# Splitting the head weights of the next phases ahead of time, and keeping the parts in DRAM

## The chip, the cores and the metric

The kernel runs on one core of one Trainium2 chip, in one launch. The metric is the device time of an execution, in microseconds (us). Beside the time there is one profiled execution, whose span is read through its page and its trace. The engines are PE (TensorE), DVE (VectorE), ACT (ScalarE), POOL (GpSimd) and SP (SyncE, which issues the transfers here).

## What is computed

Two layers of a decoder trunk, each made of feed-forward, mixer, feed-forward: six sub-layers on 512 tokens of 1024 features, all in float32. Each has the same frame, and the modulation (shift, scale, gate) comes from a product of a conditioning vector with `ada_w`:

```python
def _sublayer(x, fn, pre_g, post_g, shift, scale, gate, res_w):
    h = _rmsnorm(x, pre_g) * (1.0 + scale[:, None, :]) + shift[:, None, :]
    y = _rmsnorm(fn(h), post_g)
    return x + res_w * (1.0 + gate[:, None, :]) * y
```

`fn` is `(silu(h @ w1) * (h @ w3)) @ w2` with 2816 hidden features in the feed-forwards, a recurrence beside a convolution in the first layer's mixer (AB), and spatial gating in the second's (C). So two norms stand between any two sub-layers: one of the output, one of the sum that it is added to.

## The kernel before

**Phases.** The six sub-layers are phases 0 to 5: FFN, mixer AB, FFN, FFN, mixer C, FFN. Features lie on the partitions in eight tiles of 128 (`KT`), the 512 tokens on the free axis. PE multiplies in a 32-bit form of fewer mantissa bits, so each float32 product is made of three (`mm3`, L252 to L256): high part of the weight by high part of the value, low by high, high by low.

**Weights.** Each weight tile is loaded whole by SP's queue into one of four `raw` buffers (`fetch_w`, L228 to L231), and split on the chip into a high part (`wh`, ACT, L236) and a low part (`wl`, usually DVE, L237). There are eight buffers of each part. SP's queue works in the order in which the transfers were written.

**A feed-forward.** 22 pairs of hidden tiles in three chunks of 7, 7 and 8 (`CHUNKS`); after each chunk the products with w2 (`down`). A pair ends with its evacuation (L453 to L455, then the split at L246 and L247). Beside the products, *background jobs* run: one of the list `bg` in each *slot* (`run_bg`, called after a weight tile of a pair and after each w2 tile), and what is left at the end of the phase's body at once. Before, they are all blocks of the modulation: a load of 128x1024 of `ada_w` into a `raw` buffer and a DVE product with sum (`ada_block`, L136 to L138). There are 56 in phase 0, 24 in phase 2, 48 in phase 3.

**A change of phase.** The last seven output tiles of a phase are made in two halves of 256 tokens (`tail`), so that the norms of the first half run beside the products of the second. The norms are a chain (`chain`, L340 on): sums of squares (squares on ACT, L319; additions on GpSimd, L323, the last ones on DVE, L321), a product that gives the statistic (L287), the inverse root on DVE (L264 to L277, eight small operations), a product that spreads it over the partitions (L297), the scaled output (L354) added to x (L361), and then the same again for the next norm, up to h in two parts (L332 to L334). PE's own order is fixed, so that at each of these products it waits if DVE is late. Then the *head* of the next phase: its first three pairs of products (in C all of its first product), contraction tile by tile, on each half. The head's eight weight tiles (128x768, in C 128x1024) are fetched and split at the change itself, each as soon as PE releases buffers of the tail. The low parts of tiles 0 and 4 to 7 (`HP`) are split by GpSimd; those of 1 to 3 by DVE as "fills" at three places of the chain (`FILL`): behind the first spread, between the last two late additions, behind the second statistic.

Of the kernel before, what the change touches and what calls it, by code (L numbers as in the profile page):

```python
# [33 lines left out]
# AB: how long its steps wait, in microseconds of products; the output gates come after these square roots  # L34
# [4 lines left out]
# between phases: contraction tiles of the next weights split on GpSimd, splits that fill the gaps of the  # L39
# norms' chain (DVE, GpSimd), lag of the low parts, additions of squares that DVE takes, waits  # L40
HP = (0, 4, 5, 6, 7)
FILL, FILLG = (1, 1, 1, 0), (1, 2)
# [3 lines left out]
# start: products that warm the array, where c is spread, contraction tiles taken part by part  # L46
# [23 lines left out]
def trunk_kernel(ctx: ExitStack, tc: tile.TileContext, a: dict, out: bass.AP):  # L70
# [5 lines left out]
    ps = ctx.enter_context(tc.tile_pool(name="ps", bufs=1, space=bass.MemoryType.PSUM))  # L76

# [93 lines left out]
    def run_bg(n=1):  # L171
        for _ in range(n):
            if bg:
                if fence[0] is None:
                    bg.pop(0)()
                else:
                    with tc.issue_after(fence[0]):
                        bg.pop(0)()

# [1 line left out]
    class Flow:  # L181
        def __init__(self):
            self.t, self.gens, self.fills, self.pool, self.busy = 0.0, [], [], [], False
# [32 lines left out]
        def fill(self, n=1, m=0):  # L216
            for q, c in ((self.fills, n), (self.pool, m)):
                for _ in range(c):
                    if q:
                        q.pop(0)[1]()  # L220
# [11 lines left out]

    def split_w(raw, cols, eng):
        wh = sb.tile([P, 1024], F32R, tag="wh", bufs=8, name=nm("wh"))
        wl = sb.tile([P, 1024], F32R, tag="wl", bufs=8, name=nm("wl"))
        S.activation(wh[:, :cols], raw[:, :cols], AF.Copy)  # L236
        low = lambda e: e.tensor_tensor(wl[:, :cols], raw[:, :cols], wh[:, :cols].bitcast(F32), op=SUB)  # L237
        if eng in (1, 2):
            (flow.fills if eng == 1 else flow.pool).append((wh, lambda: low(V if eng == 1 else G)))
        else:  # L240
            low(eng)
        return wh, wl
# [17 lines left out]
    def rsqrt(src, scale):  # L260
        # first guess from the exponent bits, then a quartic in its residue
# [18 lines left out]
    # per token 1 / sqrt(mean over features + eps), on every partition  # L280
# [23 lines left out]
    class SumSq:  # L304
        # sums of squares over the feature tiles; the last ones wait for finish()
# [954 lines left out]
```

## Time and profile before

| | |
|---|---|
| three runs | 1930.12, 1931.41 (median), 1934.15 us |
| the profiled execution, its span | 1934.6 us |
| instructions | 24434 |
| DMA, mean over the span | 129 GB/s |
| read from HBM, written | 245.59 MB, 2.10 MB |

The profiled execution gives its span, and this lies 3.2 us above the median of the runs. A row of a profile names the line, the engine, the operation, and the output and inputs by their names in the program; "mm<-hid,wh" is a product into the PSUM tile `mm`. In brackets stands the time for which the engine was idle before the row, and what ended that. PE's rows overlap, so that their distance, and not their length, is the time that each takes. "PEclk" is the share of PE's full clock that was granted.

### The profile page before, as it was taken

How to read it: one execution, taken by the hardware profiler on the slowest of the kernel's cores; microseconds unless marked ns; L12 is line 12 of the kernel's file. 1: busy time of each engine (PE TensorE's matmuls, PEld its weight loads, DVE VectorE, ACT ScalarE, POOL GpSimd, SP SyncE). 2: the span in 40 equal slices, each digit the busy share in tenths (PEclk: the TensorE clock that was granted, in tenths of full speed). 3: DMA queues.
4: the chain of work that ended last, by engine and by line, in shares of the span. 5: the costliest groups of instructions: out<-in, count | busy, mean ns of one | idle time of the engine just before them, and what ended most of it. 6: DMA issues, size and time to landing. Idle time of an engine off the chain costs nothing.

```text
span 1934.6 us, 24434 instructions
## 1 busy us (share of the span) xinstructions
PE 1856.5 (96%) x9534; PEld 1567.5 (81%) x9534; DVE 1144.1 (59%) x1951; ACT 659.4 (34%) x1008; POOL 239.3 (12%) x200
## 2 busy tenths in 40 slices
PE   8999999988889999999989999999899999999997
PEld 5788888987568978888889788888878898888887
DVE  7985664687975775433367755553786483243334
ACT  3332222346755332222233322222334452222221
POOL 3200000237504000000040000000400410000002
PEclk8999999999889999999999999999999999999998
DMA  8486663421122286233222865643214132323311
GB/s 310 155 286 196 195 200 117 139 84 65 33 96 89 77 275 201 84 106 98 82 63 83 283 209 174 203 156 99 77 55 131 51 109 93 104 83 108 98 44 44
DMA packets 73125, 249.28 MB, mean 129 GB/s; under 512 B 8113, under 2 KB 10289, under 8 KB 73010
## 3 DMA queue, kind: packets, MB, share of 16 engines
q1 hardware_dynamic: 73010, 247.72, 39.3%
q8 instruction: 75, 1.23, 0.3%
q14 instruction: 40, 0.33, 0.1%
HBM read 245.59 MB, written 2.10 MB: 128 GB/s over the span
## 4 chain that ended last, share of the span: by engine, by line
PE 77%; DVE 13%; DMA 4%; ACT 3%; issue 2%; POOL 1%; SPq 0%; DVEq 0%; ACTq 0%; POOLq 0%
PE mm L256 24%; PE mm L254 24%; PE mm L255 24%; DMA raw<-in_w_dram 1%; DMA raw<-in_w13r_dram 1%; DVE wl L237 1%; DVE acc L321 1%; DVE ad L138 1%; DVE hl L334 1%; ACT wh L236 1%; PE st L297 1%; POOL hid L651 1%; POOL acc L323 1%; DVE mm L663 1%; DVE y L354 1%
## 5 line engine op out<-in xcount | busy, mean ns | idle before, releaser
L254 PE MATMUL mm<-hh,wh 128*128 128x512 f32 (+1 forms) x1734 | 644.2, 372 | 4.8 <-ACT hh L333 4.8
L256 PE MATMUL mm<-hl,wh 128*128 128x512 f32 (+1 forms) x1734 | 639.6, 369 | 0.6
L255 PE MATMUL mm<-hh,wl 128*128 128x512 f32 (+1 forms) x1734 | 637.8, 368 | 0.0
L236 ACT ACTIVATE wh<-raw 128x1024 fp32r<-128x1024 f32 (+2 forms) x310 | 313.8, 1012 | 512.0 <-PE mm L256 273.1
L254 PE MATMUL mm<-hid,wh 128*128 128x256 f32 (+1 forms) x1164 | 390.6, 336 | 5.2 <-ACT hid L246 3.3
L255 PE MATMUL mm<-hid,wl 128*128 128x256 f32 (+1 forms) x1164 | 387.9, 333 | 0.0
L256 PE MATMUL mm<-hid,wh 128*128 128x256 f32 (+1 forms) x1164 | 386.8, 332 | 0.2 <-DVE hid L247 0.2
L237 DVE TENSOR_TENSOR wl<-raw,wh 128x1024 fp32r<-128x1024 f32 (+2 forms) x277 | 327.5, 1183 | 99.7 <-ACT wh L236 98.3
L254 PEld LDWEIGHTS mm<-hh,wh 128*128 128x128 f32 x1734 | 327.5, 189 | 64.1 <-ACT hh L333 6.0
L255 PEld LDWEIGHTS mm<-hh,wl 128*128 128x128 f32 x1734 | 326.7, 188 | 60.1 <-issue 2.1
L256 PEld LDWEIGHTS mm<-hl,wh 128*128 128x128 f32 x1734 | 327.0, 189 | 58.7 <-DVE hl L334 1.9
L254 PEld LDWEIGHTS mm<-hid,wh 128*128 128x128 f32 x1164 | 223.6, 192 | 29.1 <-ACT hid L246 4.3
L256 PEld LDWEIGHTS mm<-hid,wh 128*128 128x128 f32 x1164 | 223.4, 192 | 23.4 <-DVE hid L247 1.2
L255 PEld LDWEIGHTS mm<-hid,wl 128*128 128x128 f32 x1164 | 223.8, 192 | 21.3
L138 DVE SCALAR_TENSOR_TENSOR raw<-raw,cb 128x1024 f32<-128x1024 f32 x128 | 156.1, 1223 | 139.1 <-DMA raw<-in_ada_w_dram 138.9
L237 POOL TENSOR_TENSOR wl<-raw,wh 128x768 fp32r<-128x768 f32 (+1 forms) x33 | 76.7, 2325 | 1091.4 <-ACT wh L236 794.7
L323 POOL TENSOR_TENSOR acc<-acc,tmph 128x256 f32<-128x256 f32 x112 | 90.4, 812 | 529.0 <-ACT tmph L319 521.8
L454 DVE SCALAR_TENSOR_TENSOR tmp<-tmp,mm 128x512 f32<-128x512 f32 x78 | 53.5, 686 | 147.3 <-ACT tmp L453 147.2
L455 DVE SCALAR_TENSOR_TENSOR tmp<-tmp,mm 128x512 f32<-128x512 f32 x78 | 53.5, 686 | 131.7 <-PE mm L256 131.4
L453 ACT ACTIVATE tmp<-mm 128x512 f32<-128x512 f32 x78 | 46.5, 596 | 243.1 <-PE mm L256 243.1
L482 DVE TENSOR_TENSOR y<-y,mm 128x256 f32<-128x256 f32 (+1 forms) x92 | 48.0, 522 | 123.5 <-PE mm L256 123.4
L651 POOL TENSOR_TENSOR hid<-hid,cp 128x507 f32<-128x507 f32 (+10 forms) x44 | 67.2, 1529 | 58.8 <-ACT cp L650 56.2
(204 smaller groups left out, 1317.0 us busy)
## 6 DMA issues: line engine op xcount, KB each, us to landing
raw<-in_w13r_dram SPq DMA_DIRECT2D x150, 512.0 KB, 3.8
raw<-in_ada_w_dram SPq DMA_DIRECT2D x128, 512.0 KB, 4.2
raw<-in_w_dram SPq DMA_DIRECT2D x64, 448.0 KB, 3.9
raw<-in_w_dram SPq DMA_DIRECT2D x32, 512.0 KB, 3.5
raw<-in_w13h_dram SPq DMA_DIRECT2D x24, 384.0 KB, 3.0
ad<-in_ada_w_dram SPq DMA_DIRECT2D x16, 512.0 KB, 7.2
raw<-in_ab_r_dram SPq DMA_DIRECT2D x10, 512.0 KB, 3.5
raw<-in_w13h_dram SPq DMA_DIRECT2D x8, 512.0 KB, 6.9
```

What stands on the lines that cost most here:

```text
L138: V.scalar_tensor_tensor(w, w, 0.5, cb, op0=MUL, op1=MUL, accum_out=modc[:, i : i + 1])
L236: S.activation(wh[:, :cols], raw[:, :cols], AF.Copy)
L237: low = lambda e: e.tensor_tensor(wl[:, :cols], raw[:, :cols], wh[:, :cols].bitcast(F32), op=SUB)
L254: PE.matmul(o, lhsT=wh, rhs=hi, start=start, stop=False, skip_group_check=shared)
L255: PE.matmul(o, lhsT=wl, rhs=hi, start=False, stop=False, skip_group_check=shared)
L256: PE.matmul(o, lhsT=wh, rhs=lo, start=False, stop=stop, skip_group_check=shared)
L323: G.tensor_tensor(self.acc, self.acc, t, op=ADD)
L453: S.activation(t, g, AF.Tanh, scale=0.5)
L454: V.scalar_tensor_tensor(t, t, 1.0, g, op0=ADD, op1=MUL)
L455: V.scalar_tensor_tensor(t, t, 0.5, u, op0=MUL, op1=MUL)
L482: V.tensor_tensor(self.ys[f][:, lo:hi], self.ys[f][:, lo:hi], o, op=ADD)
L651: G.tensor_tensor(ap[:, s:], ap[:, s:], q[:, s:], op=ADD)
```

## The change

A class `Ready` gives each head two steps. `prepare` returns eight background jobs; each loads a weight tile of the head, splits it (ACT and DVE, as for any weight) and stores both parts into tiles in DRAM. `bring(k)` loads the two parts of tile k from there into `wh` and `wl` buffers. Phase 0 prepares the heads of 1 and 2, phase 2 that of 3, phase 3 those of 4 and 5 (`KEEP`). At a change no weight is split: the fills, the list `HP`, and GpSimd's part are gone. The head of phase 0 is still split at the start, on GpSimd.

The jobs of a phase are merged evenly (`merge`), and spread evenly over its slots (`set_slots`), so that some slots take two. Some blocks of the modulation move to other phases (`MODS`): phase 0 has 48 blocks and 16 prepared tiles over 46 slots, phase 2 has 32 and 8 over 48, phase 3 has 40 and 16 over 48, phase 5 has 8 blocks. The rest of the diff takes comments away. Its core:

```diff
+MODS = {0: ((1, (1, 0, 2)), (2, (1, 0))), 2: ((2, (2,)), (3, (1, 0, 2))), 3: ((4, (1, 0, 2)), (5, (1, 0))), 5: ((5, (2,)),)}
+KEEP = {0: (1, 2), 2: (3,), 3: (4, 5)}
+def merge(*lists):
+    return [x for _, _, x in sorted(((i + 0.5) / len(v), n, x) for n, v in enumerate(lists) for i, x in enumerate(v))]
...
-    def run_bg(n=1):
-        for _ in range(n):
+    def run_bg(every=False):
+        n, total, i = bgn
+        bgn[2] = i + 1
+        k = len(bg) if every else max(0, len(bg) - total * max(0, n - i - 1) // n)
+        for _ in range(k):
...
-        if eng in (1, 2):
-            (flow.fills if eng == 1 else flow.pool).append((wh, lambda: low(V if eng == 1 else G)))
-        else:
-            low(eng)
+        eng.tensor_tensor(wl[:, :cols], raw[:, :cols], wh[:, :cols].bitcast(F32), op=SUB)
...
-        sq.finish(lambda: flow.fill(FILL[1]))
-        flow.fill(0, FILLG[1])
+        sq.finish()
...
+    class Ready:
+        def prepare(self):
+            self.kept = {}
+            def job(k):
+                cols = self.cols
+                w = load_w(self.src[k], cols)
+                d = [dram.tile([P, cols], F32, tag=nm("kept"), name=nm("kept")) for _ in range(2)]
+                for i in range(2):
+                    nc.sync.dma_start(d[i], w[i].bitcast(F32)[:, :cols])
+                self.kept[k] = d
+            return [lambda k=k: job(k) for k in range(KT)]
+        def bring(self, k):
+            self.w[k] = t_w()
+            for i in range(2):
+                nc.sync.dma_start(self.w[k][i].bitcast(F32)[:, : self.cols], self.kept[k][i])
...
-        for m in {0: (1, 2), 2: (3,), 3: (4, 5)}.get(n, ()):
-            bg.extend(ada_jobs(m, (1, 0, 2)))
+        jobs = [ada_jobs(m, typs) for m, typs in MODS.get(n, ())] + [phases[m].head.prepare() for m in KEEP.get(n, ())]
+        bg.extend(merge(*jobs))
...
                 if units:
-                    split_next(units.pop(0))
+                    nxt.head.bring(units.pop(0))
```

PE's instructions and their order are the same in both kernels. On the other engines, three places. DVE at the first change of phase, from an addition of the tail (L482, after the change L506) to the first step of the second inverse root (L264, after L274); `acc` are the sums of squares. Before:

```order
L482 TENSOR_TENSOR y_567<-y_567,mm_2989 128x256
L321 TENSOR_TENSOR acc_2923<-acc_2923,tmph_3006 128x256
L321 TENSOR_TENSOR acc_2923<-acc_2923,tmph_3019 128x256
L237 TENSOR_TENSOR wl_2938<-raw_2636,wh_2937 128x768
L321 TENSOR_TENSOR acc_2923<-acc_2923,tmph_3028 128x256
L482 TENSOR_TENSOR y_568<-y_568,mm_3039 128x256
L264 TENSOR_SCALAR sm_3086<-st_3083 128x2
```

And in the changed kernel, where the late additions are at L331:

```order
L506 TENSOR_TENSOR y_569<-y_569,mm_3112 128x256
L331 TENSOR_TENSOR acc_3048<-acc_3048,tmph_3129 128x256
L331 TENSOR_TENSOR acc_3048<-acc_3048,tmph_3142 128x256
L331 TENSOR_TENSOR acc_3048<-acc_3048,tmph_3151 128x256
L506 TENSOR_TENSOR y_570<-y_570,mm_3161 128x256
L274 TENSOR_SCALAR sm_3207<-st_3204 128x2
```

The split of a low part is gone from between the additions.

DVE in phase 0, at the end of the first chunk: the last operations ahead of the split of the seventh pair's hidden tile (L247, after the change L257). L138 (L145) is a block of the modulation, L237 (L251) a weight's low part, L455 (L479) the pair's evacuation; the rows with small columns are constants of mixer AB. Before:

```order
L237 TENSOR_TENSOR wl_927<-raw_924,wh_926 128x896
L149 SCALAR_TENSOR_TENSOR drv<-modc,vec 128x8
L138 SCALAR_TENSOR_TENSOR raw_953,modc<-raw_953,cb 128x1024
L151 TENSOR_SCALAR drv<-drv 128x8
L599 TENSOR_TENSOR de<-de,dr 128x4
L603 TENSOR_SCALAR di<-di 128x4
L455 SCALAR_TENSOR_TENSOR tmp_787<-tmp_787,mm_760 128x512
L237 TENSOR_TENSOR wl_959<-raw_956,wh_958 128x896
L247 TENSOR_TENSOR hid_786<-tmp_787,hid_785 128x512
```

And in the changed kernel:

```order
L628 TENSOR_SCALAR di<-di 128x4
L640 TENSOR_SCALAR dn<-vec 128x4
L251 TENSOR_TENSOR wl_906<-raw_903,wh_905 128x896
L145 SCALAR_TENSOR_TENSOR raw_932,modc<-raw_932,cb 128x1024
L479 SCALAR_TENSOR_TENSOR tmp_795<-tmp_795,mm_768 128x512
L251 TENSOR_TENSOR wl_938<-raw_935,wh_937 128x768
L257 TENSOR_TENSOR hid_794<-tmp_795,hid_793 128x512
```

A block of the modulation (raw_932) and the low part of a tile of mixer AB's head (raw_935, which row 128x768 shows) now stand there.

SP's queue in phase 0, about where that chunk's w2 tiles are loaded, with what each transfer waits for on other engines. Before, a block and a weight take turns:

```order
L137 DMA raw_953<-in_ada_w_dram 128x1024 [waits DMAHW5_49,DVE_49]
L230 DMA raw_956<-in_w_dram 128x896 [waits DMAHW2_49,DVE_49]
L137 DMA raw_985<-in_ada_w_dram 128x1024 [waits DMAHW7_49,DVE_49]
L230 DMA raw_988<-in_w_dram 128x896 [waits DMAHW4_49,DVE_49]
L137 DMA raw_1017<-in_ada_w_dram 128x1024 [waits DMAHW1_49,DVE_49]
L230 DMA raw_1020<-in_w_dram 128x896 [waits DMAHW6_49,DVE_49]
```

In the changed kernel the loads of the heads (`ab_h`, `w13h`) and the stores of their parts (`kept`) stand among them:

```order
L144 DMA raw_932<-in_ada_w_dram 128x1024 [waits DVE_49]
L239 DMA raw_935<-in_ab_h_dram 128x768 [waits DMAHW7_49,DMAHW3_49,DVE_49]
L239 DMA raw_945<-in_w_dram 128x896 [waits DVE_49]
L239 DMA raw_974<-in_w13h_dram 128x768 [waits DMAHW5_49,DMAHW1_49,DVE_49]
L404 DMA kept_941<-wh_937 128x768 [waits DMAHW2_49,Activation_49]
L404 DMA kept_942<-wl_938 128x768 [waits DVE_49]
L239 DMA raw_984<-in_w_dram 128x896 [waits DMAHW4_49]
L404 DMA kept_980<-wh_976 128x768 [waits Activation_49]
L404 DMA kept_981<-wl_977 128x768 [waits DMAHW6_49,DVE_49]
L144 DMA raw_1013<-in_ada_w_dram 128x1024 [waits DMAHW7_49]
```

The stores of a tile stand two loads behind the load of the tile, and wait for ACT's and DVE's split of it; the loads written after them are issued after them.

More of the change, by code (lines that the diff above doesn't have):

```diff
@@ L38 @@
 GSQ = {2, 3}
-HP = (0, 4, 5, 6, 7)
-FILL, FILLG = (1, 1, 1, 0), (1, 2)
 HLAG = 2
@@ L169, in set_fence, with set_slots @@
         fence[0] = next(i for i in reversed(nc.cur_bb.bb.instructions) if i.engine == nc.vector.engine)
-    def run_bg(n=1):
-        for _ in range(n):
-            if bg:
-                if fence[0] is None:
+    bgn = [0, 0, 0]
+    def set_slots(n):
+        bgn[:] = [n, len(bg), 0]
+    def run_bg(every=False):
[3 more added lines that the diff above has]
+        for _ in range(k):
+            if fence[0] is None:
+                bg.pop(0)()
+            else:
+                with tc.issue_after(fence[0]):
                     bg.pop(0)()
-                else:
-                    with tc.issue_after(fence[0]):
-                        bg.pop(0)()
     class Flow:
         def __init__(self):
-            self.t, self.gens, self.fills, self.pool, self.busy = 0.0, [], [], [], False
+            self.t, self.gens, self.busy = 0.0, [], False
         def tick(self, dt):
@@ L214, in until @@
             self.busy = False
[L216 to L220, printed above, removed]
     flow = Flow()
@@ L231, in fetch_w, with t_w @@
         return raw
+    def t_w():
+        return (
+            sb.tile([P, 1024], F32R, tag="wh", bufs=8, name=nm("wh")),
+            sb.tile([P, 1024], F32R, tag="wl", bufs=8, name=nm("wl")),
+        )
     def split_w(raw, cols, eng):
-        wh = sb.tile([P, 1024], F32R, tag="wh", bufs=8, name=nm("wh"))
-        wl = sb.tile([P, 1024], F32R, tag="wl", bufs=8, name=nm("wl"))
+        wh, wl = t_w()
         S.activation(wh[:, :cols], raw[:, :cols], AF.Copy)
-        low = lambda e: e.tensor_tensor(wl[:, :cols], raw[:, :cols], wh[:, :cols].bitcast(F32), op=SUB)
-        if eng in (1, 2):
-            (flow.fills if eng == 1 else flow.pool).append((wh, lambda: low(V if eng == 1 else G)))
-        else:
-            low(eng)
+        eng.tensor_tensor(wl[:, :cols], raw[:, :cols], wh[:, :cols].bitcast(F32), op=SUB)
         return wh, wl
@@ L323, in add, with finish @@
                 G.tensor_tensor(self.acc, self.acc, t, op=ADD)
-        def finish(self, between=lambda: None):
+        def finish(self):
             while self.queue:
-                if len(self.queue) == 1:
-                    between()
                 self.queue.pop(0)[1]()
@@ L922, in __init__ @@
             self.pr = [None] * KT
-        def fetch(self, k):
-            self.raw[k] = fetch_w(a["c_v"][k], 1024)
-        def split(self, k, eng):
-            self.w[k] = split_w(self.raw.pop(k), 1024, eng)
         def mm(self, lo, hi):
@@ L1104, in trunk_kernel @@
     set_fence()
-    bg.extend(ada_jobs(0, (2,)))
-    def done(head, k):
-        while any(x is head.w[k][0] for x, _ in flow.fills):
-            flow.fill()
-        while any(x is head.w[k][0] for x, _ in flow.pool):
-            flow.fill(0, 1)
     for n, ph in enumerate(phases):
         last = n == len(phases) - 1
-        for m in {0: (1, 2), 2: (3,), 3: (4, 5)}.get(n, ()):
-            bg.extend(ada_jobs(m, (1, 0, 2)))
+        if n == 0:
+            bg.extend(ada_jobs(0, (2,)))
+        jobs = [ada_jobs(m, typs) for m, typs in MODS.get(n, ())] + [phases[m].head.prepare() for m in KEEP.get(n, ())]
+        bg.extend(merge(*jobs))
         eng = {"P": nc.tensor.engine, "A": nc.scalar.engine, "V": nc.vector.engine, "G": nc.gpsimd.engine}
@@ L1119, in trunk_kernel @@
             ph.rest()
-        run_bg(100)
+        run_bg(every=True)
         nxt = None if last else phases[n + 1]
@@ L1125, in trunk_kernel @@
         with tc.manual_schedule(engines={nc.tensor.engine, nc.vector.engine}):
-            fetched = 0
-            def split_next(k):
-                nonlocal fetched
-                if last:
-                    return
-                while fetched < min(KT, k + 4):
-                    nxt.head.fetch(fetched)
-                    fetched += 1
-                if k >= 0:
-                    nxt.head.split(k, 2 if k in HP else 1)
-            split_next(-1)
             free = 8 - len(ph.wt)
-            units = list(range(KT))
-            for k in range(free):
-                split_next(units.pop(0))
+            units = [] if last else list(range(KT))
+            for k in range(0 if last else free):
+                nxt.head.bring(units.pop(0))
             for step in ph.tail(0):
@@ L1150, in trunk_kernel @@
                 if units:
-                    split_next(units.pop(0))
+                    nxt.head.bring(units.pop(0))
             while units:
-                split_next(units.pop(0))
+                nxt.head.bring(units.pop(0))
             def second_half():
@@ L1165, in trunk_kernel @@
                 if k < KT:
-                    done(nxt.head, k)
                     flow.until(first, lambda: have[0] > k)
```

12 lines of the change are left out of this document (6 added, 6 removed).

## The prediction

> **What bounds the kernel now.** I began with the page's first lines and the busy time of each engine in stretches cut at the phases.
>
> ```profile
> span 1934.6 us, 24434 instructions
> PE 1856.5 (96%) x9534; PEld 1567.5 (81%) x9534; DVE 1144.1 (59%) x1951; ACT 659.4 (34%) x1008; POOL 239.3 (12%) x200
> ```
>
> TensorE (PE) is busy 96% of the span, so 1934.6 − 1856.5 = 78 us at most can be won by waiting less. The table by stretches shows where those lie (columns: stretch, its length, then busy time of PE, PEld, DVE, ACT, POOL, granted clock, DMA share, GB/s):
>
> ```profile
> 70.00:360.00 290.00, 290.00 (x1281) 237.23 (x1280) 189.05 (x312) 87.11 (x112) 0.00 (x0) 1.00 0.62 201
> 360.00:440.00 80.00, 74.48 (x599) 73.48 (x598) 52.95 (x136) 28.72 (x59) 25.79 (x25) 0.96 0.25 80
> 570.00:660.00 90.00, 82.44 (x625) 79.29 (x626) 56.83 (x130) 40.17 (x85) 25.52 (x25) 0.94 0.24 77
> 960.00:1045.00 85.00, 77.10 (x623) 75.78 (x622) 56.12 (x137) 31.58 (x65) 25.64 (x25) 0.98 0.20 61
> 1045.00:1340.00 295.00, 294.46 (x1299) 240.36 (x1298) 171.37 (x241) 85.84 (x111) 0.00 (x0) 1.00 0.59 189
> 1340.00:1430.00 90.00, 83.38 (x529) 75.33 (x528) 60.96 (x146) 30.31 (x60) 30.02 (x27) 0.96 0.16 53
> 1500.00:1590.00 90.00, 82.96 (x668) 81.50 (x668) 58.30 (x132) 42.40 (x90) 26.48 (x25) 0.98 0.25 76
> ```
>
> The feed-forward bodies (first and fifth row) leave PE no idle time. The five changes of phase (the other rows) leave 5.52 + 7.56 + 7.90 + 6.62 + 7.04 = 34.6 us, at a clock below 1.00; the start, mixer AB and the end hold the rest, which the change doesn't touch. PE's waits, summed by what it waited for:
>
> ```profile
> PE st L297 <- DVE sm L277: 17.2, 9, 3.7
> PE st L287 <- DVE acc L321: 14.9, 9, 3.5
> PE mm L254 <- ACT hh L333: 4.8, 5, 1.1
> PE mm L254 <- ACT hid L774: 1.9, 1, 1.9
> ```
>
> Nearly all of it is the norms' chain: the statistic waits for the last additions of squares (L321), its broadcast for the inverse root (L277). At the third change, PE's and then DVE's rows (start, length, bracketed idle time before):
>
> ```profile
> 1000.24 0.58 PE L287 MATMUL st<-ones,acc 128*128 128x1 f32 x4 [2.47 <-DVE acc L321]
> 1005.96 1.20 PE L297 MATMUL st<-ident,sm 128*128 128x128 f32 x4 [2.92 <-DVE sm L277]
> ```
>
> ```profile
> 985.85 0.16 DVE L274 SCALAR_TENSOR_TENSOR sm<-sm 128x2 f32<-128x2 f32 x1
> 988.50 0.42 DVE L361 TENSOR_TENSOR x<-x,y 128x256 f32<-128x256 f32 x1
> 995.92 2.96 DVE L321 TENSOR_TENSOR acc<-acc,tmph 128x256 f32<-128x256 f32 x2 [0.30 <-POOL acc L323]
> 998.81 0.95 DVE L237 TENSOR_TENSOR wl<-raw,wh 128x768 fp32r<-128x768 f32 x1
> 1002.23 1.42 DVE L274 SCALAR_TENSOR_TENSOR sm<-sm 128x2 f32<-128x2 f32 x1
> 1004.08 1.74 DVE L277 SCALAR_TENSOR_TENSOR sm<-sm,sm 128x2 f32<-128x2 f32 x1
> ```
>
> GpSimd meanwhile:
>
> ```profile
> 990.22 5.67 POOL L323 TENSOR_TENSOR acc<-acc,tmph 128x256 f32<-128x256 f32 x6 [1.83 <-ACT tmph L319]
> 995.86 1.88 POOL L237 TENSOR_TENSOR wl<-raw,wh 128x768 fp32r<-128x768 f32 x1
> 1001.77 1.86 POOL L237 TENSOR_TENSOR wl<-raw,wh 128x768 fp32r<-128x768 f32 x1
> 1004.00 1.80 POOL L237 TENSOR_TENSOR wl<-raw,wh 128x768 fp32r<-128x768 f32 x1 [0.36 <-ACT wh L236]
> ```
>
> Each long DVE row starts under a GpSimd split: L274 takes 0.16 us at 985.85 but 1.42 under the split of 1001.77, and ends with it; so does L277 (1.74) under that of 1004.00; two additions that began at 995.92 take 2.96 under that of 995.86 and an addition behind it. So the chain is late by splits of weights twice over: GpSimd's hold DVE up, and DVE's own (0.95) stands between two additions.
>
> The idle costs a second time, in the clock. The stretches granted half of it, one at each change:
>
> ```profile
> 395.20:402.00 6.80, 6.26 (x30) 0.52 0.53 165
> 620.50:627.30 6.80, 5.50 (x26) 0.52 0.45 145
> 1006.20:1009.60 3.40, 3.40 (x18) 0.53 0.61 177
> 1385.00:1391.90 6.90, 5.71 (x28) 0.52 0.30 105
> 1545.50:1548.90 3.40, 3.40 (x19) 0.53 0.61 175
> 1029.00:1036.00 7.00, 5.75 (x46) 1.00 0.00 0
> ```
>
> PE works 6.26 + 5.50 + 3.40 + 5.71 + 3.40 = 24.3 us there at half speed, and loses 12.1. The last row holds a wait of 1.1 us (L333) that didn't trip it.
>
> **The change, part by part.** *Idle at the changes.* The splits leave the changes. PE's order is the same. Of the 34.6 us, 4.8 (L333: h itself must come), 1.9 (L774, end of mixer AB) and some 0.6 of small gaps stay: 27.3 can go. What is late next? DVE's late additions without the lock: GpSimd's six end at 990.22 + 5.67 = 995.89, then three of 0.41 to 0.43 give 997.2, before 1000.24 − 2.47 = 997.77, where PE asks. So that wait ends, with 0.6 us to spare; a GpSimd addition of the second half in that place (5.67 / 6 = 0.94) would take 0.3 of it back. The root's eight operations at their free lengths take about 2 us; PE has products for as long (from 1000.24 to 1005.96 − 2.92 = 1003.04, 2.8 us). So that wait ends too. I take −27.3; at worst, were each of the ten or so waits still late by 0.5, −22.
>
> *Clock.* With only 1.1 us waits left, which the last row shows harmless: −12.1. At worst it stays (−0). The Trainium skill ("TensorE: Matmul & The Clock Gate", Part 1) says that the rate halves after a whole idle window of about 3.4 us. By it only the second and the fourth change, with waits over 3.4 us, would have tripped, and the gain would be half of 5.50 + 5.71, 5.6 us, not 12.1. The trace differs: 2.47 and 2.92 us tripped the third.
>
> *Weights brought at the change.* Each tile is now two loads of 384 KB (512 for mixer C) straight into the buffers that PE has just released. The raw loads of such a size, a body with its DMA queues full, and two of PE's products in the tail:
>
> ```profile
> raw<-in_w13h_dram SPq DMA_DIRECT2D x24, 384.0 KB, 3.0
> 100.00:140.00 40.00, 40.00 (x175) 1.00 0.85 295
> ```
>
> ```profile
> 1009.45 0.28 PE L254 MATMUL mm<-hid,wh 128*128 128x256 f32 x1
> 1010.75 0.28 PE L256 MATMUL mm<-hid,wh 128*128 128x256 f32 x1
> ```
>
> Eleven products from the one to the other make 0.118 us each. The tail frees a buffer every 24 products, 2.8 us, so 2 × 393 KB / 2.8 = 281 GB/s are wanted, under 295; for C 2 × 524 / 2.8 = 374, so there seven tiles lag by 0.7 us each, some 5 us. The head takes a tile in 18 products, 2.1 us (C's are larger), so the last tile is asked for 7 × 2.1 = 15 us after the tail, with 5 + 3 us needed: no wait; 0 to +6.
>
> *Background work in the bodies.* DVE takes 40 splits there that it or GpSimd did at the changes (40 × 0.95 to 1.2) and phases 0 and 3 each hand eight reductions on: (1.23 each, by the row of 713.06 below). Phase 0: 16 × 0.95 − 8 × 1.23 = +5 us on 189 of 290: DVE isn't the bound. ACT is at 87 of 290. The loads are nearer to theirs. Phase 0 moved 201 GB/s × 290 us = 58 MB. Now go 8 reductions (−4.2) and come 16 loads (+6.3) and 32 stores (+12.6): 73 MB, 252 GB/s, against 295. Phase 3 (56 MB) goes to −4.2 + 8 × (0.52 + 0.39) + 16 × (0.52 + 0.39): 73 MB too, 249 GB/s. Slot by slot: phase 0's 46 slots each take one unit's weights, 48/46 reductions and 16/46 tiles of 0.75 + 1.5 loads' worth, 1 + 1.04 + 0.78 = 2.8 loads (2.7 with a w2 unit's 0.875), at 0.52 MB / 295 = 1.78 us 5.0 (4.8) us. PE's unit is 24 (21) products of 0.233 us by the rows of 106.31 below, 5.6 (4.9) us. So loads keep up, just so in the w2 stretches, and where they fall behind DVE stands at a reduction whose data isn't there. Such an event is in the trace, at the end of the first chunk of phase 2:
>
> ```profile
> 713.06 1.23 DVE L138 SCALAR_TENSOR_TENSOR raw<-raw,cb 128x1024 f32<-128x1024 f32 x1 [1.77 <-DMA raw<-in_ada_w_dram]
> 715.61 0.64 PE L254 MATMUL mm<-hid,wh 128*128 128x512 f32 x1 [2.98 <-ACT hid L246]
> ```
>
> The evacuation waits behind the reduction, PE 2.98 us for it, and then works 3.4 us at half clock (another 1.7): 4.7 us an event. In phase 2 the new order has two loads fewer ahead of that evacuation: I take −2.5 (−4.7 to 0). Phase 0's first chunk is where it is closest:
>
> ```profile
> 109.98 0.68 DVE L247 TENSOR_TENSOR hid<-tmp,hid 128x512 fp32r<-128x512 f32 x1
> 106.31 0.40 PE L254 MATMUL mm<-hid,wh 128*128 128x512 f32 x1
> 108.17 0.39 PE L256 MATMUL mm<-hid,wh 128*128 128x512 f32 x1
> ```
>
> Eight products lie between these two, 0.233 us each. PE needs the value after six of the chunk's seven tiles, 18 products after 106.31, at 110.5, just as L247 ends it (110.6). The new order puts one load more ahead (1.8 us), so an event there: +4.5 (0 to +10). Stores wait in SP's queue for ACT's and DVE's split, and the loads behind them start later by about 1.5 us for each pair of tiles; the lead of the loads covers it, but I put +1 (0 to +10) on phases 0 and 3 together. The Trainium skill ("DMA: Bandwidth & Descriptors", Anatomy of one DMA) speaks against the change here: the completion of a transfer that writes to HBM comes late, most of 2 us. By it each prepared tile would hold its two ring buffers that much longer. No store of this kind stands in the trace, so no row shows it.
>
> *Sum:* 1934.6 − 27.3 − 12.1 − 2.5 + 4.5 + 1 + 0 = 1898.2. The median of the runs, 1931.41, lies 3.2 below the profiled span (0.17%), so a run may show 1895; I keep 1898.
>
> **The rivals.** *(A) Forecast:* chain free, clock kept, bodies hold, 1886 to 1908 (low end: −27.3 − 12.1 − 4.7 − 3.2 = 1887; high end: phase 0 and the chain at their worse values). Chance 0.66.
>
> *(B) Half of it:* the waits shrink but each change keeps one near 1 to 2 us, because with less idle PE reaches each later step of the chain sooner, or brought tiles are late; then the clock still halves. 1934.6 − 22 = about 1912, with phase 0's event 1917. For it: 2.46 us was enough at the first change. Against: the spare time worked out above, and 1.1 us harmless. By the Trainium skill's rule of the clock, above, the time would be about 1905. Chance together 0.20.
>
> *(C) Slower: the queue of stores starves the bodies.* SP works in order; a store of a low part waits for DVE's split, which stands behind a reduction, which waits for a load behind an earlier store. Each such knot makes an event like that at 715.61, 4.7 us. There are 40 prepared tiles, in about 24 groups. From 39.4 / 4.7 = 8 events the gain is gone; with 12 the time is 1898 + 56 − 4.5 = about 1950. For it: 252 of 295 GB/s as a mean leaves 15%, the loads of w2 stretches are at their limit, and stores may move slower than loads, for which there is no row. Against: after 140 us the loads were ahead of the splits. Chance 0.10: 0.07 of it slower, the rest with so few events that they only eat the gain.
>
> *(D) The splits were hidden anyway,* or the chain is held by GpSimd's additions as well: 1934 less a few. The rows of 2.96, 1.42 and 1.74 on the path speak against it. Chance 0.04, one half of it within no change, the other a little faster.
>
> **How the numbers follow.** Within 0.2%, 3.9 us, this kernel can't be told from itself. Faster: A 0.66, B 0.20, D 0.02 and 0.01 of C (few events), 0.89. Same: 0.02 of C and 0.02 of D, 0.04. Slower: the rest of C, 0.07. The range reaches from the best sum to the poorer cases of B, 1886 to 1920; C and D lie outside it.
>
> **What would show it.** Right: PE's waits on L287 and L297 at changes fall from 32 us to under 6, no half clock between 370 and 1560 at the changes, GpSimd without splits after the start, additions and roots of DVE at 0.16 and 0.42. Wrong: PE idle inside 70 to 360 or 1045 to 1340 for more than 15 us in place of about 0, waits on loads at the heads, or a row of half clock at each change as before.

## The result and the profile after

| | before | after |
|---|---|---|
| runs, median | 1931.11 us (1930.12 to 1934.15, 4 runs) | 1902.22 us (1900.13 to 1905.42, 4 runs) |
| ratio of the runs | | 0.9846, 95% interval 0.9832 to 0.9859 |
| profiled execution, span | 1934.6 us | 1901.0 us |
| written to HBM | 2.10 MB | 35.65 MB |

The changed kernel is faster by 1.5%, 28.9 us between the medians and 33.6 between the two profiled spans. The forecast was 1898, with 1886 to 1920 as the range. A run is reported 1.7 to 1.9 us longer than its span (1902.68 against 1901.0 for the profiled one of after), so that the profiled execution of before, with a span of 1934.6, was slower than all four runs in the table. That is why the gain is larger between the spans than between the medians.

The first lines of the page after:

```profile
span 1901.0 us, 24653 instructions
PE 1845.7 (97%) x9534; PEld 1556.2 (82%) x9534; DVE 1139.7 (60%) x1976; ACT 666.7 (35%) x1008; POOL 186.9 (10%) x175
```

The table by stretches, cut as before (length, busy PE, PEld, DVE, ACT, POOL, granted clock, DMA share, GB/s):

```profile
70.00:360.00 290.00, 282.70 (x1213) 228.68 (x1213) 190.73 (x310) 99.56 (x124) 0.00 (x0) 0.99 0.75 255
360.00:440.00 80.00, 78.63 (x638) 76.85 (x637) 48.13 (x131) 25.05 (x55) 15.79 (x20) 1.00 0.33 106
570.00:660.00 90.00, 86.76 (x669) 83.10 (x668) 52.50 (x130) 37.84 (x82) 16.11 (x20) 0.98 0.38 127
960.00:1045.00 85.00, 83.65 (x659) 80.94 (x658) 57.01 (x151) 29.54 (x63) 15.02 (x19) 1.00 0.31 103
1045.00:1340.00 295.00, 295.00 (x1336) 242.72 (x1335) 172.57 (x225) 99.28 (x124) 2.43 (x4) 1.00 0.72 248
1340.00:1430.00 90.00, 89.30 (x511) 77.22 (x510) 69.08 (x189) 32.32 (x59) 14.91 (x19) 1.00 0.37 127
1500.00:1590.00 90.00, 88.69 (x600) 81.58 (x601) 65.21 (x145) 39.16 (x76) 10.75 (x13) 1.00 0.46 147
```

At the five changes PE is now idle for 1.37 + 3.24 + 1.35 + 0.70 + 1.31 = 8.0 us, where it was 34.6, and the clock is full but in the second (570 to 660 holds the end of mixer AB too, and a wait of 1.9 us there is followed by half clock in both kernels). The first row shows the price: 7.3 us of idle time in phase 0, where there was none. The waits of PE:

```profile
PE mm L264 <- ACT hid L256: 7.0, 2, 6.5
PE mm L264 <- ACT hh L341: 4.8, 5, 1.1
PE st L307 <- DVE sm L287: 4.2, 2, 2.3
PE mm L264 <- ACT hid L799: 1.9, 1, 1.9
PE st L297 <- DVE acc L331: 0.6, 1, 0.6
```

(L297 and L307 are the statistic and its spread, L287 and L297 before; L331 the late additions.) The waits for the spread that are left lie at the start and at the end. At the third change DVE's and then GpSimd's rows that answer to those of before:

```profile
988.11 1.82 DVE L331 TENSOR_TENSOR acc<-acc,tmph 128x256 f32<-128x256 f32 x3
992.07 0.16 DVE L284 SCALAR_TENSOR_TENSOR sm<-sm 128x2 f32<-128x2 f32 x1
992.65 0.16 DVE L287 SCALAR_TENSOR_TENSOR sm<-sm,sm 128x2 f32<-128x2 f32 x1
```

```profile
982.24 5.33 POOL L333 TENSOR_TENSOR acc<-acc,tmph 128x256 f32<-128x256 f32 x6 [1.50 <-ACT tmph L329]
988.84 0.80 POOL L333 TENSOR_TENSOR acc<-acc,tmph 128x256 f32<-128x256 f32 x1 [1.27 <-ACT tmph L329]
```

The steps that took 1.42 and 1.74 us take 0.16. The additions end at 989.93, and PE's statistic starts at 990.10 without a wait: the chain has some 0.2 us to spare, no more. (Three additions of 0.41 each would take 1.2 at most and not 1.82; they stand under GpSimd's own addition of 988.84.) In phase 0, DVE at the end of the second chunk, then the product of PE that waits for it, and PE's clock behind that (length, busy PE, clock, DMA share, GB/s):

```profile
221.20 1.23 DVE L145 SCALAR_TENSOR_TENSOR raw<-raw,cb 128x1024 f32<-128x1024 f32 x1 [5.45 <-DMA raw<-in_ada_w_dram]
230.71 1.23 DVE L145 SCALAR_TENSOR_TENSOR raw<-raw,cb 128x1024 f32<-128x1024 f32 x1 [2.59 <-DMA raw<-in_ada_w_dram]
232.87 0.68 DVE L479 SCALAR_TENSOR_TENSOR tmp<-tmp,mm 128x512 f32<-128x512 f32 x1
```

```profile
234.27 0.80 PE L264 MATMUL mm<-hid,wh 128*128 128x512 f32 x1 [6.46 <-ACT hid L256]
```

```profile
234.27:239.53 5.26, 5.26 (x12) 0.50 0.90 300
```

DVE stands twice at a block of the modulation whose load isn't there. The evacuation (L479) comes behind the second, PE waits 6.46 us for it, and then works 5.26 us at half clock, which costs another 2.6. Phase 2's stall of 2.98 us is gone.

### The profile page after: what moved, and what is told of

The parts are those of the page before. It is cut to its first block, busy times and chain, and to the rows that moved or that the text cites. A ratio compares the mean times of both kernels' runs of the same rounds, so it can differ in the third digit from the quotient of the medians.

```text
span 1901.0 us, 24653 instructions
## 1 busy us (share of the span) xinstructions
PE 1845.7 (97%) x9534; PEld 1556.2 (82%) x9534; DVE 1139.7 (60%) x1976; ACT 666.7 (35%) x1008; POOL 186.9 (10%) x175
## 3 DMA queue, kind: packets, MB, share of 16 engines
HBM read 279.15 MB, written 35.65 MB: 166 GB/s over the span
## 4 chain that ended last, share of the span: by engine, by line
PE 77%; DVE 11%; DMA 6%; ACT 3%; issue 2%; POOL 1%; SPq 0%; DVEq 0%; ACTq 0%; POOLq 0%
PE mm L264 24%; PE mm L266 24%; PE mm L265 24%; DMA raw<-in_w13r_dram 2%; DMA raw<-in_ada_w_dram 2%; DVE wl L251 2%; DMA raw<-in_w13h_dram 1%; ACT wh L250 1%; DMA raw<-in_w_dram 1%; DVE raw L145 1%; DVE ad L145 1%; POOL hid L676 1%; PE st L307 1%; DVE mm L688 1%; DVE wl L848 1%
## 5 line engine op out<-in xcount | busy, mean ns | idle before, releaser
L264 PE MATMUL mm<-hh,wh 128*128 128x512 f32 (+1 forms) x1734 | 644.2, 372 | 4.8 <-ACT hh L341 4.8
L251 DVE TENSOR_TENSOR wl<-raw,wh 128x1024 fp32r<-128x1024 f32 (+2 forms) x302 | 351.6, 1167 | 162.0 <-ACT wh L250 152.1
L264 PE MATMUL mm<-hid,wh 128*128 128x256 f32 (+1 forms) x1164 | 386.6, 332 | 8.9 <-ACT hid L256 7.0
L264 PEld LDWEIGHTS mm<-hh,wh 128*128 128x128 f32 x1734 | 327.1, 189 | 63.7 <-ACT hh L341 6.0
L264 PEld LDWEIGHTS mm<-hid,wh 128*128 128x128 f32 x1164 | 219.9, 189 | 32.9 <-ACT hid L256 8.0
L266 PEld LDWEIGHTS mm<-hid,wh 128*128 128x128 f32 x1164 | 219.7, 189 | 23.8 <-DVE hid L257 1.7
L265 PEld LDWEIGHTS mm<-hid,wl 128*128 128x128 f32 x1164 | 219.8, 189 | 21.3
L145 DVE SCALAR_TENSOR_TENSOR raw<-raw,cb 128x1024 f32<-128x1024 f32 x128 | 155.7, 1221 | 71.7 <-DMA raw<-in_ada_w_dram 71.0
L506 DVE TENSOR_TENSOR y<-y,mm 128x256 f32<-128x256 f32 (+1 forms) x92 | 48.1, 523 | 134.7 <-PE mm L266 134.4
L479 DVE SCALAR_TENSOR_TENSOR tmp<-tmp,mm 128x512 f32<-128x512 f32 x78 | 53.5, 686 | 111.1 <-PE mm L266 110.7
L329 ACT ACTIVATE tmph<-y 128x256 f32<-128x256 f32 x84 | 35.0, 417 | 114.2 <-DVE y L506 112.7
```

The source lines that it names most:

```text
L145: V.scalar_tensor_tensor(w, w, 0.5, cb, op0=MUL, op1=MUL, accum_out=modc[:, i : i + 1])
L251: eng.tensor_tensor(wl[:, :cols], raw[:, :cols], wh[:, :cols].bitcast(F32), op=SUB)
L264: PE.matmul(o, lhsT=wh, rhs=hi, start=start, stop=False, skip_group_check=shared)
L265: PE.matmul(o, lhsT=wl, rhs=hi, start=False, stop=False, skip_group_check=shared)
L266: PE.matmul(o, lhsT=wh, rhs=lo, start=False, stop=stop, skip_group_check=shared)
L479: V.scalar_tensor_tensor(t, t, 0.5, u, op0=MUL, op1=MUL)
```

## The experiments

Each comparison is with runs of the kernel before on the same chip. The theory is that of the prediction: GpSimd's splits, reading SBUF, hold up DVE's operations of the norms' chain; that wait and the half clock behind it go with them. Rivals: that DVE's own fills made the chain late, that GpSimd's queue did, and that the half clock has another cause. A run with two executions has a wide interval, so the ratios of e1, e2 and e3b are known to about 4 us each way.

| run | median | ratio to before, 95% | profiled span |
|---|---|---|---|
| after | 1902.22 | 0.9846 (0.9832 to 0.9859) | 1901.0 |
| e1_gp_reads | 1922.78 | 0.9944 (0.9921 to 0.9966) | 1919.8 |
| e2_gp_memory_fill | 1903.34 | 0.9843 (0.9821 to 0.9865) | 1900.4 |
| e3_dve_fills | 1928.15 | 0.9974 (0.9963 to 0.9986) | 1923.0 |
| e3b_dve_fills_const | 1903.43 | 0.9855 (0.9836 to 0.9875) | 1901.5 |
| e10_both | 1931.73 | 0.9994 (0.9971 to 1.0016) | 1926.5 |
| e4_before_spin | 1929.99 | 0.9980 (0.9970 to 0.9989) | 1928.8 |
| e9_bodies | 1940.53 | 1.0045 (1.0030 to 1.0060) | 1935.4 |
| e5_pace | 1929.43 | 0.9986 (0.9974 to 0.9999) | 1929.3 |
| e11_no_store | 1937.52 | 1.0022 (1.0009 to 1.0035) | 1935.7 |
| e6_store_gpsimd | 1930.47 | 0.9996 (0.9987 to 1.0005) | 1928.4 |
| e12_one_list | 1906.71 | 0.9859 (0.9844 to 0.9874) | 1902.3 |
| e13_quiet_ends | 1900.54 | 0.9837 (0.9812 to 0.9863) | 1898.1 |

A run's whole time mixes the changes of phase with the stall in phase 0, and that differs from profile to profile: in after, e1, e2, e3, e3b, e10 and e9, whose phase 0 is the same program, PE's wait there was 3.7 to 6.5 us. So here is the profiled execution of some runs, cut at the same PE instructions in each (the first to start after 70, 360, 440, 570, 660, 960, 1045, 1340, 1430, 1500 and 1590 us in the profile of before), in us:

| run | five changes together | body of phase 0 | of phase 2 | of phase 3 |
|---|---|---|---|---|
| before | 433.5 | 289.9 | 299.9 | 295.1 |
| after | 393.7 | 300.8 | 295.4 | 293.9 |
| e1_gp_reads | 419.1 | 296.7 | 296.8 | 293.9 |
| e2_gp_memory_fill | 395.0 | 299.6 | 295.5 | 293.9 |
| e3b_dve_fills_const | 397.6 | 298.2 | 296.7 | 293.9 |
| e10_both | 422.3 | 299.3 | 295.1 | 293.9 |
| e9_bodies | 430.2 | 299.6 | 296.5 | 293.9 |
| e11_no_store | 426.7 | 291.9 | 298.6 | 302.0 |
| e13_quiet_ends | 393.9 | 291.8 | 300.1 | 296.2 |

**GpSimd's work put back (e1, e2).** The five operations of e1, appended when a tile is brought and taken out where the old splits were:

```diff
+            v = self.w[max(0, k - 2) if k in HP else k]
+            def extra(e):
+                o = t_tmp().bitcast(mybir.dt.bfloat16)
+                e.tensor_tensor(o[:, :768], v[0].bitcast(F32)[:, :768], v[1].bitcast(F32)[:, :768], op=SUB)
+            if k in HP:
+                flow.pool.append((self.w[k][0], lambda: extra(G)))
```

In e2 `extra` is a copy of one column and four memory fills of a 128x512 tile.

> The changed kernel (span 1901.0 us, 0.6 us of waits on the chain at its changes of phase) with five dead GpSimd operations put back at each change, at the places of the old splits: each reads two weight tiles of 128x768 and writes a temporary that nobody reads. Lock theory (a GpSimd operation that reads SBUF holds up DVE's operations with two SBUF inputs): DVE's additions and root steps grow again to 1.4 to 3 us, PE's waits on L287/L297 of before return to 12 to 25 us, with half clock behind them: span 1918 to 1938. Rival one (DVE's own fills made the chain late): no change, 1899 to 1906. Rival two (GpSimd's queue: its own additions come late behind the splits): time as in the lock theory, but DVE's rows stay at 0.16 and 0.42.

> As e1_gp_reads, but each of the five operations is a copy of one column and four memory fills of 128x512, which read nothing. Lock theory in its strict form (only a GpSimd operation that reads SBUF holds DVE up): DVE's rows stay at 0.16 and 0.42, span 1899 to 1908. Theory that any GpSimd activity blocks DVE, or that GpSimd's queue is what is late: 1912 to 1938; the two are told apart by DVE's rows.

e1 lost 19 us against after by the ratios. Between the two profiles its five changes lost 25.4 us, and its phase 0 happened to be 4.1 us shorter. Its rows on DVE and GpSimd at the third change:

```profile
992.48 3.41 DVE L339 TENSOR_TENSOR acc<-acc,tmph 128x256 f32<-128x256 f32 x3 [0.30 <-POOL acc L341]
997.66 0.34 DVE L288 TENSOR_SCALAR sm<-sm,sm 128x1 f32<-128x1 f32 x2
998.03 1.37 DVE L292 SCALAR_TENSOR_TENSOR sm<-sm 128x2 f32<-128x2 f32 x1
```

```profile
992.41 1.80 POOL L432 TENSOR_TENSOR tmp<-wh,wl 128x768 bf16<-128x768 f32 x1
997.57 1.82 POOL L432 TENSOR_TENSOR tmp<-wh,wl 128x768 bf16<-128x768 f32 x1
```

The additions take 3.41 in place of 1.82, and the root's step 1.37 in place of 0.16, both under a GpSimd operation. The step before it (L288), which takes one tile and a value for each partition, runs under the same operation in its usual 0.34. In e2 GpSimd is occupied for longer, and DVE runs on:

```profile
991.38 2.28 POOL L434 MEMSET tmp<- 128x512 f32 x4
```

```profile
992.53 0.16 DVE L292 SCALAR_TENSOR_TENSOR sm<-sm 128x2 f32<-128x2 f32 x1
992.73 0.16 DVE L293 SCALAR_TENSOR_TENSOR sm<-sm,sm 128x2 f32<-128x2 f32 x1
```

Four fills, 2.28 us in all, and the same step takes its 0.16 under them; the time is that of after. PE's waits on the chain at the changes are 1.9 us in all here (15.5 in e1, 0.6 in after). So it isn't that GpSimd is busy, and its queue makes little of it: its reading is what holds DVE up. The Trainium skill ("SBUF — State Buffer", the section "SBUF: two separate sides") says that DVE's operations with two SBUF inputs wait only for a GpSimd operation that reads SBUF. The trace agrees: the step takes 1.37 us under the reading operation and 0.16 under the fills.

**DVE's fills put back (e3, e3b).** The same `extra`, run on DVE for the tiles 1 to 3, in e3 with the brought tile as input, in e3b with the constant `cb`.

```diff
+            else:
+                flow.fills.append((self.w[k][0], lambda: extra(V)))
```

> The changed kernel with the three DVE operations of each change put back as dead work (128x768, 0.95 us), at the places of the old fills: behind the first spread, between the last two late additions, behind the second statistic. Lock theory: only the one between the additions counts, 0.95 against 0.6 us of spare time, so 0.3 to 0.5 us at each change and no half clock: span 1901 to 1905. Rival (the fills were the larger part of the late chain): waits of 10 us and more, half clock, 1912 to 1930.

e3's span is 22 us longer than after's, as the rival had it, but not for its reason. Its first fill of the first change:

```profile
389.67 0.96 DVE L432 TENSOR_TENSOR tmp<-wh,wl 128x768 bf16<-128x768 f32 x1 [2.54 <-DMA wh<-kept]
```

It waits 2.54 us for the brought tile, and the whole chain stands behind it in DVE's order: PE's wait for the additions is 3.44, 3.14, 3.32, 4.20 and 2.50 us at the five changes. That is a fault of this experiment (the old fills read tiles that had landed), so it was made again without the wait.

> e3_dve_fills again, the three dead DVE operations reading a constant tile, so that none of them waits for a transfer (in e3_dve_fills the first stood 2.54 us for a brought tile, with the chain behind it). Lock theory: 0.95 and what it adds to the additions against 0.6 us of spare time, 0.3 to 1.5 us at each change, at most one or two half clocks: span 1902 to 1909. Rival (the fills alone made the chain late): 15 us and more, as in e3_dve_fills, 1916 to 1930.

e3b is as fast as after by the ratios: waits of 0.83 us at three changes, 0.35 and 0.22 at the others, and the clock of after at all five. Its changes are 3.9 us longer than after's, which its shorter phase 0 hides. So the fills alone cost some 4 us, without the clock.

**Both put back (e10).** The operations of e1 and of e3b in one kernel.

> The changed kernel with both sorts of dead work at each change: the five GpSimd operations of e1_gp_reads and the three of DVE from e3b_dve_fills_const. If the two together were what the change took away, the waits on the chain come back whole: 25 us and more on the two lines of the chain, half clock at each change, span 1928 to 1938 (the kernel before had 1934.6, with about 4 us less in the bodies). If GpSimd alone mattered, as e1_gp_reads and e3b_dve_fills_const taken one by one say: 1919 to 1923. So a sum larger than the parts shows DVE's splits to cost where GpSimd's stand beside them.

29 us came back in the ratio (0.9994 against 0.9846), where the ratios of the parts give 19 and 2: an excess of 8 us, hardly more than the noise of four ratios. The changes by themselves show none: they are 28.6 us longer than after's, against 25.4 and 3.9 for the parts. So the two add up, and in the profiles the excess lies in phase 0, where e1 and e3b happened to stall less. At the third change DVE's and GpSimd's rows:

```profile
997.81 1.49 DVE L432 TENSOR_TENSOR tmp<-cb 128x768 bf16<-128x768 f32 x1
999.22 2.02 DVE L339 TENSOR_TENSOR acc<-acc,tmph 128x256 f32<-128x256 f32 x1
1003.38 1.38 DVE L292 SCALAR_TENSOR_TENSOR sm<-sm 128x2 f32<-128x2 f32 x1
1004.79 1.74 DVE L293 SCALAR_TENSOR_TENSOR sm<-sm,sm 128x2 f32<-128x2 f32 x1
```

```profile
998.44 2.52 POOL L432 TENSOR_TENSOR tmp<-wh,wl 128x768 bf16<-128x768 f32 x1
1002.91 3.60 POOL L432 TENSOR_TENSOR tmp<-wh,wl 128x768 bf16<-128x768 f32 x2
```

The fill puts the last addition under GpSimd's operation (2.02), and what comes later meets the next ones (1.38, 1.74). But the waits did not come back whole: PE waits 17.6 us on the chain's two lines at the changes, where before had 28.0, and the span of 1926.5 lies between the two ranges that were expected. The four profiles with the old changes (before, e9, e5, e11) need 426.7 to 433.5 us for the five, e10 422.3. So 4 to 11 us of the old changes are not in the dead work. The raw loads, ACT's splits there and mixer C's wider tiles (128x1024) are left out of it; none was put back by itself, and which of them it is stays open.

**The clock (e4).** The kernel before, with four dead products in front of the second statistic and of its spread:

```diff
+        for _ in range(n):
+            PE.matmul(o[:, 256:512], lhsT=ones, rhs=cb[:, 0:256], start=True, stop=True, skip_group_check=True)
```

> The kernel before (profiled 1934.6, runs 1931), with four dead products of 256 columns put in front of the second statistic and in front of its spread, in the first half of each change of phase, so that PE works where it waited. Their results are never read. Theory that the half clock comes from PE's idle time: no row of half clock at the changes, 12 us less loss, against some 2 us for products where the wait was shorter than they: time down by 8 to 12 us, 1919 to 1924 in runs. Rival (the clock halves for another reason, such as the load at the changes): time same or up by 2 to 6 us.

The changes of phase in its table by stretches (busy PE, clock, DMA share, GB/s):

```profile
360.00:440.00 80.00, 75.75 (x622) 1.00 0.22 74
570.00:660.00 90.00, 85.99 (x664) 0.98 0.25 81
960.00:1045.00 85.00, 80.73 (x654) 1.00 0.20 63
1340.00:1430.00 90.00, 84.14 (x519) 0.96 0.15 47
1500.00:1590.00 90.00, 86.33 (x682) 1.00 0.26 86
```

Before, these read 0.96, 0.94, 0.98, 0.96 and 0.98. The half clock is gone from all changes but that to mixer C (where a wait of 2.64 us is left; what the second row still has follows the end of mixer AB), while the loads are those of before: it does come from PE's idle time. The time fell by 4 us in the ratio, not 8 to 12. The dead products take 1.89 us at a place, ten times 18.9 us in all, and PE still waits 16.8 us on the chain: 35.7 us in place of the 28.0 that PE waited on it before (13.1 for the root, 14.9 for the additions), which eats most of what the clock gave.

**The bodies alone (e9, e5, e11).** e9 has the new bodies and the old changes: the tiles are prepared and stored, and never brought. e5 has the new list and pace of blocks, and no prepared tiles (`KEEP = {}`). e11 is e9 without the two stores.

```diff
-                for i in range(2):
-                    nc.sync.dma_start(d[i], w[i].bitcast(F32)[:, :cols])
```

> The bodies of the changed kernel with the changes of phase of the kernel before: all background jobs, the splits and stores ahead of time too, in the new order and number, but the stored parts are never read, and the heads are fetched and split at the change as before. Theory that the new bodies cost what phase 0 shows (6.5 us of waiting at 228, about 3 of half clock) and give back phase 2's 4.7: 3 to 7 us slower than before, 1934 to 1939 in runs, and all waits of the chain as before. Rival (the bodies cost nothing, the profile's stall was one execution's): 1926 to 1931.

> The kernel before with the new list and pace of modulation blocks alone (no splits ahead of time, no stores; changes of phase as before). If phase 2's stall (2.98 us and 1.7 of half clock) went because of the new order of loads, it goes here too and phase 0 stays without a stall: 1925 to 1929 in runs. If it went by chance, or because of the prepared tiles: 1930 to 1934.

> e9_bodies (the new bodies with the old changes, 1940.5 in runs) without its 80 stores: the head tiles are loaded and split in the bodies, but kept nowhere. Theory that the stores, through bandwidth and through the part buffers that they hold, make the new bodies slow: 1927 to 1933. Rival (loads and splits are enough to starve them, four raw buffers being the limit): 1936 to 1941.

e9 is 0.45% slower than before, 8.7 us (5.8 to 11.6 by the interval), a little over what was expected. Set against after, which has the same bodies, it gives the changes of phase by themselves: 1.0045 − 0.9846 is 38 us; by the profiles of before and after they are 39.8 us shorter. e5 lost its stall in phase 2 (2.98 to 0.83 us) but got one of 2.52 in phase 3; it is 2.7 us faster, between what the two theories gave. e11 is 4.4 us faster than e9 by the ratios, whose intervals overlap, and at 1937.5 it lies in the range of the rival. Without the stores PE is idle for 1.1 us in phase 0 where e9 had 5.6, but phase 3 has a stall of 4.5 with 3.3 of half clock: its body of phase 0 is 7.7 us shorter than e9's and that of phase 3 is 8.0 longer. So the stores are needed for phase 0's stall, but that they make up a part of what the bodies cost as a whole isn't shown.

**Phase 0's stall (e6, e12, e13).** Three ways to take it away: the stores from GpSimd's queue (`nc.gpsimd.dma_start`), the tiles of two heads in one list, and no jobs in the four slots ahead of a chunk's end:

```diff
-            set_slots(2 * (NPAIR - self.j0 - len(CHUNKS)) + 2 * KT)
+            w = []
+            for c, (j0, j1) in enumerate(CHUNKS):
+                n = 2 * (j1 - 1 - max(j0, self.j0))
+                w += [0 if c < 2 and n - i <= 4 else 1 for i in range(n)] + [1] * (KT if c < 2 else 0)
+            set_slots(w)
```

> The changed kernel with the stores issued from GpSimd's queue, which has nothing else to do in the bodies, so that no load stands behind a store. Theory that the order in SP's queue made the 6.5 us stall in phase 0 (a load issued late behind a store that waits for a split): the stall shrinks to under 2 us, 1893 to 1898 in runs. Rival one (four raw buffers and the latency of a load limit the flow): same stall, 1899 to 1904. Rival two (such stores cost more, or GpSimd's part of issuing them holds DVE up): slower than 1904.

The stall doubled, to 12.8 us, and others came at the ends of chunks in phases 2 (4.3 and 2.0) and 3 (10.2); the gain was gone. What its page and after's page say of the stores:

```profile
kept<-wh POOLq DMA_DIRECT2D x32, 384.0 KB, 5.1
kept<-wl POOLq DMA_DIRECT2D x32, 384.0 KB, 6.5
```

```profile
kept<-wh SPq DMA_DIRECT2D x32, 384.0 KB, 3.4
kept<-wl SPq DMA_DIRECT2D x32, 384.0 KB, 3.7
```

(last number: us from issue to landing.) Nothing held the loads back for the stores any more, and the stores took longer, while each held its part buffer. ACT's waits show that (columns: us in total, times, longest), in after and then in e6:

```profile
ACT wh L250 <- DMA kept<-wh: 45.4, 17, 5.2
```

```profile
ACT wh L250 <- DMA kept<-wh: 72.3, 16, 6.8
```

So taking the stores out of SP's order doesn't take the stall away. What that order costs by itself isn't shown, since the stores took longer at the same time. The second part of rival two can be told: GpSimd takes 0.55 us to issue a store, but DVE's operations in phase 0 are as long as in after (a block's product 1.22 us in both), so that issuing didn't hold DVE up. Whether bandwidth or the held buffers weigh more in e6 stays open.

> The changed kernel with the tiles of two heads in one list, so that in phases 0 and 3 they are spread one by one, where the changed kernel puts them in pairs into the same slots (two loads of a head, four stores). Theory that the stall in phase 0 is made by such a pair, whose loads and stores hold up the load that DVE's next block waits for: the stall at 228 falls from 6.5 to under 3 us and its half clock goes with it, 1895 to 1899 in runs. Rival (the rate over the whole phase is what lacks, whatever the order): within 2 us of the changed kernel, 1900 to 1904.

The theory of the pairs fell: the stall stayed (7.86 us), and the time, 1906.7, is no better than after's.

> The changed kernel with no background job in the four slots ahead of the end of a feed-forward's first and second chunk; the other slots take that many more (the same jobs, in the same order). Theory that the stall of phase 0 at 228 comes from a load that DVE's next block waits for, with the evacuation of the chunk's last pair behind it on DVE: without blocks there the loads are ahead, the stall falls from 6.5 to under 2 us and its half clock goes, 1892 to 1897 in runs. Rival (the phase as a whole lacks loads, so that the stall only moves into the fuller slots behind): 1899 to 1906 and PE idle by 4 us or more elsewhere in phase 0.

DVE at the same place in e13, and the body of phase 0 as the table has it:

```profile
224.79 1.22 DVE L145 SCALAR_TENSOR_TENSOR raw<-raw,cb 128x1024 f32<-128x1024 f32 x1
225.94 0.69 DVE L255 TENSOR_TENSOR hid<-tmp,hid 128x512 fp32r<-128x512 f32 x1
233.72 1.23 DVE L145 SCALAR_TENSOR_TENSOR raw<-raw,cb 128x1024 f32<-128x1024 f32 x1 [4.59 <-DMA raw<-in_ada_w_dram]
```

```profile
70.00:360.00 290.00, 289.18 (x1273) 235.33 (x1273) 192.37 (x313) 99.35 (x127) 0.73 (x1) 1.00 0.76 258
```

Here the evacuation (L255) is done at 226.6 and the long wait for a load (4.59) comes behind it, where PE has w2 products to do: idle time in phase 0 falls from 7.3 to 0.8 us at the same traffic (258 GB/s). So at the same mean rate the place of the late load, ahead of an evacuation or behind it, decides whether it costs PE 7 us or almost nothing. But phase 2 got a stall of 3.25 us and phase 3 one of 1.68 at the end of their first chunks, and the whole, 1900.5, is within the noise of after and above the 1892 to 1897 that were expected. Quiet ends in phase 0 alone weren't tried.

## Why the prediction came out as it did

**Idle at the changes, −27.3.** Right: 26.6 by the tables, and of PE's waits on the chain 0.6 us is left, at the change to mixer C. (The 32 us of waits that the prediction names hold 4.1 at the start and the end; 28.0 stood at the changes.) The spare time was 0.2 us, near the 0.3 that it left after a GpSimd addition. e1, e2, e3b and e10 show the cause and set the weights: GpSimd's reading alone makes the changes 25.4 us longer, DVE's fills alone 3.9, both 28.6, the clock included. The prediction put the two side by side as two delays; they add up as such, but GpSimd's is by far the larger. The 4 to 11 us that are missing to the old changes have no cause shown.

**Clock, −12.1.** Right: no half clock is left at the changes, and e4 shows that idle time makes it. In e1 waits of 2.6 to 3.2 us tripped it at the changes; those of 0.8 us in e3b and of 1.1 us everywhere did not. Both sums together were 39.4; the five changes are 39.8 us shorter between the profiles of before and after, and the same bodies with old and new changes differ by 38 in the runs (e9 against after).

**Tiles brought late, 0 (to +6).** Right: PE waits at no head for a load.

**Phase 2, −2.5.** More: the stall and its half clock went whole, 4.7. In e9 0.7 us of it was left, in e13 it was back with 3.25, so which phase has a stall turns on small shifts of the order.

**Phases 0 and 3, +4.5 and +1.** This is the term that was mis-sized, and its place was wrong. The prediction looked at the end of the first chunk, by counting the loads ahead of the evacuation; there PE waited 0.52 us. The stall came at the end of the second chunk, 6.46 us and 2.6 of half clock, 9.6 us with the first. The prediction had the mechanism (a block at the head of DVE's queue whose load is late, as at 715.61 before) and the rate (252 GB/s forecast, 255 measured), but took the backlog to be greatest at the start. In the table by PE instructions phase 0 is 10.9 us longer and phase 3 is 1.2 shorter, +9.7 where +5.5 was forecast. With phase 2's −4.5 the bodies cost 5.2 us by the profiles, where 3 was forecast; by the runs of e9 they cost 8.7 (5.8 to 11.6). A run varies by some 3 us around its median, so that these hardly differ. The late end of writes that the prediction feared isn't borne out for stores from SP's queue, which landed sooner than the loads beside them (last section).

**The rivals.** B (waits of 1 to 2 us left, clock still halved) did not come, and C did only as one event; e6 shows what C looks like, 29 us of stalls. The measured median is 4 us over the forecast. In spans, in which the sum was made, it is 2.8 us (1901.0 against 1898.2), a gain of 33.6 where 36.4 was forecast: the changes came as forecast, and the bodies cost some 2 us more. A part of the nearness is luck. Phase 2 gave back 2 us more than forecast, against some 4 more that phases 0 and 3 cost. And the prediction knew that before's profile lay above its runs, yet kept 1898 where its own correction gave 1895; between the runs the gain was 28.9, 7.5 less than the sum.

**The clock's threshold.** The waits of 2.6 to 3.2 us in e1 go with a granted clock of 0.96 to 0.98 in its five changes, where after has 1.00 in four. At the third change, a wait of PE and the stretch behind it (length, busy PE, clock, DMA share, GB/s):

```profile
996.04 0.58 PE L305 MATMUL st<-ones,acc 128*128 128x1 f32 x4 [2.89 <-DVE acc L339]
```

```profile
997.50:1000.90 3.40, 3.08 (x15) 0.50 0.15 14
```

The Trainium skill ("TensorE: Matmul & The Clock Gate", Part 1) puts the threshold at a whole idle window of about 3.4 us. By e1 and by before, the traces don't agree with that threshold. The 1905 that the prediction worked out from it lies 2.8 us from the median of the runs, the forecast 4.2, but that is chance: the half clock did go from all five changes. Where the limit lies isn't shown: at the change to mixer C a wait of 2.41 us in e5 was followed by half clock, and one of 2.38 in e9 wasn't.

## What to carry to other kernels

Work that is moved off a critical chain pays twice where the chain's waits also cost the clock; price both, from the rows of the stretch. An operation on GpSimd that reads SBUF isn't free beside a chain of small DVE operations, even when both engines look idle enough: look for rows that are ten times as long as their like. And background work wants its late loads where nobody stands behind them: look at what is queued behind each wait, not only at the mean rate. Last, compare experiments stretch by stretch: the totals of e1, e3b and e10 made two costs look larger together than apart, and the stretches show that they add up.

## What the runs showed of the hardware

Four memory fills on GpSimd, 2.28 us, didn't lengthen DVE's steps (0.16), while a GpSimd operation of 1.8 us that reads did (1.37). A step with one tile as input kept its 0.34 us under the same operation. Over the five changes 25 such reading operations cost 25.4 us, the half clock behind the waits included. PE's clock was halved for 3.4 or 6.8 us behind single waits of 2.6 to 3.2 us in e1, and stayed full behind those of 0.8 and 1.1. The stores to DRAM landed in 3.2 and 3.7 us in phase 0 of after, beside loads of the same 384 KB that took 4.0 and 4.4 in the same body, so a write wasn't slower to end than a read; from GpSimd's queue they took 5.5 and 6.3 in the same body.
